# Full-array products in a two-block transformer kernel: score products with the queries' low parts on 128 rows, state products of the recurrence on 128 columns

## The chip, the cores and the metric

One core of a Trainium2 chip runs the whole program. The metric is the device time of one execution in microseconds. Three runs of the kernel before took 2723.95, 2730.51 and 2730.61 us; their median is 2730.51 us.

## The reference, cut to what matters

The network has a first block of two layers (mixers, convolutions and feed-forward nets over 512 tokens of width 1024) and a second block that mixes three things over the same 512 tokens: sparse attention with six heads in two groups (NSA), a recurrence with four heads (RWKV-7), and block attention with six heads (MoBA). All heads have 64 channels. The change touches only the second block's mixer. At 512 tokens every block is selected, so the attention parts are causal softmax attention, and NSA's window covers all tokens too.

```python
def _moba_mixer(p):
    q, k, v = [jnp.transpose(t.reshape(b, s, MOBA_HEADS, HEAD_DIM), (0, 2, 1, 3)) for t in _split_2(p, [D_MOBA] * 3)]
    ...
        s_o = jnp.einsum('bhqd,bhkd->bhqk', qc, ko)
        prob = _masked_softmax(jnp.concatenate([s_g, s_o], axis=-1) * scale, mask).astype(v.dtype)
        return jnp.einsum('bhqk,bhqkd->bhqd', prob[..., :n_g], vg) + jnp.einsum('bhqk,bhkd->bhqd', prob[..., n_g:], vo)
...
def _rwkv7_mixer(p, mu, w0, w2, a0, a2, g2, k_k, k_a, r_k, lnx_w, lnx_b):
    ...
    def step(state, inp):
        r_t, w_t, k_t, v_t, kk_t, a_t = inp
        sa = jnp.einsum('bhvk,bhk->bhv', state, -kk_t)
        state = state * w_t[:, :, None, :] + sa[..., None] * (kk_t * a_t)[:, :, None, :] + v_t[..., None] * k_t[:, :, None, :]
        return state, jnp.einsum('bhvk,bhk->bhv', state, r_t)
    ...
```

Everything is in float32. The kernel reaches that precision in the large products by splitting each operand into a high part (rounded to the format that TensorE takes in one pass) and a low part (the rest).

## The kernel before

`run` goes through the stages in order: first mixer, feed-forward net, conformer, second feed-forward net, then `mixer2` (the second block's mixer), then the last feed-forward net. The query tiles of `mixer2`'s attention are made from 1922.4 us on, and its score products run from 1951.8 to 2296.2 us. In `mixer2` three generators are interleaved: the attention (`attention`, with its projections `att_ft` and `att_tok`), the recurrence (`rwkv_blocks`) and the first half of the output projection (`wout_half`). Constants such as `RW_EVERY` and `WO_SHARE` say in which proportion they are interleaved. The building framework then sets the order of each engine's instructions by costs of its own; within an engine the order is fixed in the program.

**Score products.** For a block of 128 queries (`tb` from 0 to 3) and one head, the scores over the first `w = 128 (tb + 1)` keys are three products that accumulate in one bank of PSUM (lines 1967 to 1969, in `att_unit`). A key tile holds, for one head, the high parts of the 64 channels in one half of the 128 partitions and their low parts in the other half. A query tile `qp` (made by `att_q`, lines 1852 to 1862) has 128 columns for each of two heads with the high parts of the queries in both halves, so L1967 multiplies the high queries by high and low keys at once, on all 128 rows of TensorE's array. L1968 adds the low queries times the high keys, on the 64 rows of the half that has the high keys. L1969 adds the causal mask, on 128 rows. Each `qp` tile takes two ScalarE casts (L1859), two ScalarE copies to the other half (L1860) and two GpSimd subtractions that make the low parts (L1861). There are 24 such tiles, 12 for MoBA and 12 for NSA, and 72 score groups: 18 for each width of 128, 256, 384 and 512 keys.

**The recurrence.** A block of 128 tokens is worked in two halves of 64 (`c` in `rwkv_state`). In each half four products with the state `ST` (128 rows, two pairs of heads, two left sides) write `pu`; their left side is the 64 columns of the half's tokens, so they use 64 columns of the array and write 64 partitions (L1746). VectorE makes `U` from them (L1747), ScalarE copies the output part (L1748), and then products on 64 rows add to `pSr` (L1753, L1754), from which VectorE and GpSimd make the next state (L1757, L1759).

In the names of the profile, MATMUL and LDWEIGHTS carry the part of the array that they use: 64\*128 is 64 rows and 128 columns, 128\*64 is 128 rows and 64 columns. A float32 product that is not split has two records for each instruction.

Of the kernel before, what the change touches and what calls it, by code (L numbers as in the profile page):

```python
# [17 lines left out]
P = 128  # L18
# [294 lines left out]
class Kern:  # L313
# [1386 lines left out]
    def rwkv_state(self, pr, b):  # L1700

        nc, rp = self.nc, self.rwp
        mm = nc.tensor.matmul
        V = nc.vector
        hs = [slice(0, 64), slice(64, 128)]
        hd = [(p, h) for p in range(2) for h in range(2)]
        tk = lambda nm, p, b, h, tp=slice(0, P): pr[p][4][nm][tp, b, hs[h]]
        TT, MT, PT, QT = self.inv
        if b == 0:

            self.ST = [rp.tile([P, 2, P], F32, name=f"ST{j}") for j in range(2)]
            for j in range(2):
                nc.gpsimd.memset(self.ST[j], 0.0)
            self.oall = self.wp.tile([P, 2, T], F32, name="oall", tag="wh", bufs=3)
        o5 = self.oall.rearrange("p q (b h c) -> p q b h c", b=4, h=2)

        pair = lambda t, p: t.rearrange("p (q h) c -> p q (h c)", h=2)[:, p]
        own = lambda t, h: t.rearrange("p (q h) c -> p q h c", h=2)[:, :, h, 64 * h:64 * h + 64]
        pm = self.x("pmv", (P, 4, P))
        for i, (p, h) in enumerate(hd):  # L1720
            mm(pm[:, i], MT[:, i], pr[p][4]["v"][:, b], start=True, stop=True)
        mv = rp.tile([P, 4, 64], F32, name="mv", tag="mu", bufs=1)
        for h in range(2):
            nc.scalar.copy(mv.rearrange("p (q h) c -> p q h c", h=2)[:, :, h], own(pm, h))
        p1 = self.x("pt1", (P, 2, P))
        for i, (p, h) in enumerate(hd):
            mm(p1[hs[h], p], tk("al", p, b, h), TT[:, i], start=True, stop=True)
        t1 = rp.tile([P, 2, P], F32, name="t1")
        nc.scalar.copy(t1, p1)
        p2 = self.x("pt2", (P, 4, P))  # L1730
        for i, (p, h) in enumerate(hd):
            mm(p2[:, i], TT[:, i], pair(mv, p), start=True, stop=True)
        t2 = rp.tile([P, 2, P], F32, name="t2")
        for h in range(2):
            V.tensor_copy(t2[:, :, hs[h]], own(p2, h))
        yield
        U = rp.tile([P, 2, P], F32, name="U", tag="mu", bufs=1)
        for c in range(2):
            tp = hs[c]
            ts = slice(b * P + c * 64, b * P + c * 64 + 64)  # L1740
            ST, new = self.ST
            pu = self.x("pu", (P, 2, 2, P))
            for z in range(2):
                for p in range(2):
                    l = t1[:, p, c * 64:(c + 1) * 64] if z == 0 else pr[p][0][:, 1, ts]
                    mm(pu[tp, z, p], l, ST[:, p], start=True, stop=True)  # L1746
            V.scalar_tensor_tensor(U[tp], pu[tp, 0], -1.0, t2[tp], op0=OP.mult, op1=OP.add)  # L1747
            nc.scalar.copy(o5[tp, :, b].rearrange("p q h c -> p q (h c)"), pu[tp, 1])  # L1748
            if b < 3 or c < 1:
                pS = self.x("pSr", (P, 2, P))  # L1750
                for p in range(2):
                    tok = pr[p][4]
                    mm(pS[:, p], tok["kt"][tp, b], tok["v"][tp, b], start=p == 0, stop=False, skip_group_check=True)  # L1753
                    mm(pS[:, p], tok["b"][tp, b], U[tp, p], start=False, stop=p == 1, skip_group_check=True)  # L1754
                sw = rp.tile([P, 2, 64], F32, name="sw")
                for h in hs:
                    V.tensor_add(sw[h], ST[h, :, h], pS[h, :, h])  # L1757
                for h, e in zip(hs, (V, nc.gpsimd)):
                    e.tensor_mul(new[h, :, h], sw[h], self.wc[h, :, 2 * b + c:2 * b + c + 1].to_broadcast([64, 2, 64]))  # L1759
                self.ST = [new, ST]  # L1760
            yield
        po = self.x("po", (P, 4, P))
        for i, (p, h) in enumerate(hd):
            mm(po[:, i], QT[:, i], pr[p][4]["v"][:, b], start=True, stop=False)
            mm(po[:, i], PT[:, i], U[:, p], start=False, stop=True)
        for h in range(2):
            V.tensor_add(o5[:, :, b, h], o5[:, :, b, h], own(po, h))
        yield
# [83 lines left out]
    def att_q(self, q, tile):  # L1852

        nc = self.nc
        t = tile("qp", F32R)
        for j in range(2):
            a, b = slice(64 * j, 64 * j + 64), slice(64 - 64 * j, 128 - 64 * j)
            h = slice(j * P, j * P + P)
            nc.scalar.copy(t[a, h], q[a])  # L1859
            nc.scalar.copy(t[b, h], t[a, h])  # L1860
            nc.gpsimd.tensor_sub(t[a, 2 * P:3 * P], q[a], t[a, h])  # L1861
        return t

    def att_tok(self, part):
# [85 lines left out]
    def att_unit(self, tb, qk, one, v, gate, out, add=False):  # L1950
# [3 lines left out]
        nc, ap = self.nc, self.attp  # L1954
        w = (tb + 1) * P
# [6 lines left out]
        for j, (q, h, k) in enumerate(qk):  # L1962
            if j == 0 or not pair:
                pt = self.acc()
            p = pt[:, j * pair * w:j * pair * w + w]
            a = slice(64 * h, 64 * h + 64)
            nc.tensor.matmul(p, q[:, h * P:h * P + P], k[:, :w], start=True, stop=False, skip_group_check=True)  # L1967
            nc.tensor.matmul(p, q[a, 2 * P:3 * P], k[a, :w], start=False, stop=False, skip_group_check=True)  # L1968
            nc.tensor.matmul(p[:, tb * P:], self.identr, self.mneg, start=False, stop=True, skip_group_check=True)  # L1969
            ps.append(p)  # L1970
            if not pair:
                nc.vector.reduce_max(mx[:, j:j + 1], p, axis=AX.X)
            elif j:
                nc.vector.reduce_max(mx, pt[:, :2 * w].rearrange("p (j w) -> p j w", j=2), axis=AX.X)
            yield 0.2 * (tb + 1)
# [14 lines left out]
        for j0 in range(0, 2, m):  # L1990
            p = self.acc()
# [5 lines left out]
            t = self.t("peT")  # L1997
# [5 lines left out]
        p = self.acc()  # L2003
        for i, (t, s) in enumerate(tt):
            j, b = divmod(i, tb + 1)
            nc.tensor.matmul(p[:, P * j:P * j + P], t[:, s], v(j, b)[0], start=i == 0, stop=i == 2 * tb + 1,  # L2006
                             skip_group_check=True)
        for j in range(2):
            o = out if one else out[:, 64 * j:64 * j + 64]
            c = P * j + v(j, 0)[1]  # L2010
            a = p[:, c:c + 64]
# [428 lines left out]
```

## Time and profile before

| what | value |
|---|---|
| median of three runs | 2730.51 us |
| profiled execution | 2720.59 us, of which the span of instructions is 2718.9 us |
| TensorE (PE) busy | 2608.4 us, 96% of the span |
| VectorE (DVE) busy | 1832.1 us, 67% |
| ScalarE (ACT) busy | 1150.7 us, 42% |
| GpSimd (POOL) busy | 784.5 us, 29% |
| mean granted TensorE clock | 0.984 |

The profile names instructions by engine, source line and tiles. PEld is the queue of TensorE's weight loads, which can run beside the products. The start of a record is when the engine took it up; the time from one start to the next is what a product costs in a stream, and it is shorter than the record's own duration, since products are pipelined.

### The profile page before, as it was taken

The numbers are of one execution on the slowest core, as the hardware profiler recorded it, in microseconds if no ns is written. First come the engines' busy times: TensorE is split into PE (matmuls) and PEld (weight loads), VectorE is DVE, ScalarE is ACT, GpSimd is POOL, SyncE is SP. The second block draws the span as 40 slices with busy tenths as digits, with TensorE's granted clock in tenths as the row PEclk, the third lists the DMA queues.
The fourth block names the chain that finished last, engine by engine and source line by source line (L and its number), as shares of the span: only waits on it lengthen the run. The fifth ranks groups of instructions, "written<-read, shape, count | busy, mean of one in ns | idle before, by whom it ended". The sixth has DMA issues, their size and how long they took to land.

```text
span 2718.9 us, 37608 instructions
## 1 busy us (share of the span) xinstructions
PE 2608.4 (96%) x14088; PEld 2178.6 (80%) x14088; DVE 1832.1 (67%) x3234; ACT 1150.7 (42%) x2072; POOL 784.5 (29%) x767
## 2 busy tenths in 40 slices
PE   7999999999999999998789999999999999999998
PEld 3877778889778888787678888888787878988887
DVE  4686775775778888768998888657534666644422
ACT  3365543333424333228656433326535334533322
POOL 2132321222343111335754311342222002322231
PEclk8999999999999999999899999999999999999999
DMA  6112115341353333841012333333223001433332
GB/s 241 49 40 70 39 55 171 124 135 45 118 177 109 98 97 105 265 142 63 31 47 63 97 98 96 91 95 104 70 73 92 17 9 55 125 93 101 91 98 75
DMA packets 89367, 255.84 MB, mean 94 GB/s; under 512 B 10336, under 2 KB 14752, under 8 KB 89184
## 3 DMA queue, kind: packets, MB, share of 16 engines
q1 hardware_dynamic: 82320, 240.51, 28.3%
q0 software_dynamic: 2112, 6.29, 0.7%
q10 hardware_dynamic: 4752, 6.63, 0.7%
q8 instruction: 111, 1.82, 0.3%
q14 instruction: 72, 0.59, 0.1%
HBM read 245.00 MB, written 7.34 MB: 93 GB/s over the span
## 4 chain that ended last, share of the span: by engine, by line
PE 79%; DVE 12%; ACT 4%; issue 3%; DMA 2%; POOL 1%; DVEq 0%; POOLq 0%; SPq 0%; ACTq 0%
PE acc L402 19%; PE acc L404 19%; PE acc L403 19%; DVE cv L1470 2%; PE pa L1152 2%; PE acc L2006 1%; DVE e L972 1%; DVE wl L393 1%; DMA adaraw<-in_ada 1%; PE acc L1881 1%; PE acc L1968 1%; PE pr L618 1%; PE acc L1995 1%; PE ptm L1695 1%; PE acc L1969 1%
## 5 line engine op out<-in xcount | busy, mean ns | idle before, releaser
L402 PE MATMUL acc<-xh,wl 128*128 128x512 f32 (+2 forms) x2056 | 778.5, 380 | 16.2 <-DVE wl L393 7.4
L404 PE MATMUL acc<-xl,wh 128*128 128x512 f32 (+2 forms) x2056 | 765.0, 375 | 3.0 <-DVE xl L724 1.3
L403 PE MATMUL acc<-xh,wh 128*128 128x512 f32 (+2 forms) x2056 | 766.3, 374 | 0.0
L394 POOL TENSOR_TENSOR wl<-wraw,wh 128x256 fp32r<-128x256 f32 (+3 forms) x330 | 355.1, 1077 | 1181.7 <-ACT wh L391 1044.0
L391 ACT CAST wh<-wraw 128x1024 fp32r<-128x1024 f32 (+3 forms) x330 | 338.7, 1028 | 552.4 <-PE acc L404 320.2
L393 DVE TENSOR_TENSOR wl<-wraw,wh 128x768 fp32r<-128x768 f32 (+3 forms) x330 | 364.3, 1105 | 178.3 <-ACT wh L391 146.5
L402 PEld LDWEIGHTS acc<-xh,wl 128*128 128x128 f32 (+1 forms) x2056 | 391.7, 191 | 81.8 <-DVE wl L393 8.9
L404 PEld LDWEIGHTS acc<-xl,wh 128*128 128x128 f32 (+1 forms) x2056 | 389.2, 191 | 74.7 <-issue 1.9
L403 PEld LDWEIGHTS acc<-xh,wh 128*128 128x128 f32 (+1 forms) x2056 | 391.9, 191 | 56.9 <-issue 1.4
L2358 DVE SCALAR_TENSOR_TENSOR cacc<-acc,pk,cacc 128x441 f32<-128x441 f32 (+2 forms) x352 | 243.6, 692 | 28.0 <-ACT cacc L2349 18.6
L402 PE MATMUL acc<-gh,wl 128*128 128x512 f32 (+1 forms) x594 | 220.2, 371 | 0.0
L404 PE MATMUL acc<-gl,wh 128*128 128x512 f32 (+1 forms) x594 | 219.2, 369 | 0.0
L403 PE MATMUL acc<-gh,wh 128*128 128x512 f32 (+1 forms) x594 | 219.1, 369 | 0.0
L655 DVE SCALAR_TENSOR_TENSOR adaacc<-adaraw,sv,adaacc 128x512 f32<-128x512 f32 x140 | 116.7, 837 | 32.0 <-DMA adaraw<-in_ada 30.0
L404 PEld LDWEIGHTS acc<-gl,wh 128*128 128x128 f32 x594 | 111.4, 188 | 21.2
L403 PEld LDWEIGHTS acc<-gh,wh 128*128 128x128 f32 x594 | 111.4, 188 | 21.0
L402 PEld LDWEIGHTS acc<-gh,wl 128*128 128x128 f32 x594 | 111.4, 188 | 21.1
L1470 DVE SCALAR_TENSOR_TENSOR cv<-up,pk,cv 128x512 f32<-128x512 f32 x104 | 121.4, 1181 | 3.7 <-ACT cv L1444 1.5
L2302 DVE SCALAR_TENSOR_TENSOR cacc<-acc,pk,cacc 128x511 f32<-128x511 f32 (+1 forms) x44 | 32.9, 749 | 70.0 <-ACT cacc L2300 69.2
L1142 ACT COPY kcur<-kk 128x512 f32<-128x512 f32 x56 | 37.3, 665 | 94.5 <-DVE kk L1166 94.4
L1152 PE MATMUL pa<-qq,kcur 128*128 128x128 f32 x448 | 64.7, 288 | 5.8 <-DVE qq L1164 5.4
L2360 ACT ACTIVATE cacc<-cacc 128x512 f32<-128x512 f32 x44 | 27.8, 632 | 95.4 <-DVE cacc L2358 95.4
(671 smaller groups left out, 4679.3 us busy)
## 6 DMA issues: line engine op xcount, KB each, us to landing
wraw<-in_wup SPq DMA_DIRECT2D x132, 512.0 KB, 3.6
adaraw<-in_ada SPq DMA_DIRECT2D x160, 256.0 KB, 3.5
wraw<-in_wdn SPq DMA_DIRECT2D x48, 512.0 KB, 3.6
wraw<-in_wc SPq DMA_DIRECT2D x24, 512.0 KB, 3.7
wraw<-in_wdn SPq DMA_DIRECT2D x24, 384.0 KB, 3.1
wraw<-in_ada SPq DMA_DIRECT2D x16, 512.0 KB, 5.4
wraw<-in_wf SPq DMA_DIRECT2D x16, 512.0 KB, 3.7
wraw<-in_wo SPq DMA_DIRECT2D x16, 512.0 KB, 3.7
```

The lines of the kernel that those rows point to most:

```text
L391: nc.scalar.copy(wh[:, :n], raw[:, :n])
L393: nc.vector.tensor_sub(wl[:, :c], raw[:, :c], wh[:, :c])
L394: nc.gpsimd.tensor_sub(wl[:, c:n], raw[:, c:n], wh[:, c:n])
L402: mm(acc, wl, xh, start=first, stop=False)
L403: mm(acc, wh, xh, start=False, stop=False)
L404: mm(acc, wh, xl, start=False, stop=last)
L655: nc.vector.scalar_tensor_tensor(a, r, self.sv[:, k, 0:1], a, op0=OP.mult, op1=OP.add)
L1142: nc.scalar.copy(t.rearrange("p (a b c) -> p a b c", b=2, c=m), self.alt(kk, 0)(m))
L1152: mm(pa[:, s], kcur[:, s], self.alt(qq, 1)(m, c * P, P), start=True, stop=True)
L1470: nc.vector.scalar_tensor_tensor(acc, up[:, j:j + T], w(j), acc, op0=OP.mult, op1=OP.add)
L2302: nc.vector.scalar_tensor_tensor(a[:, d:], pg[:, :T - d], self.col("gcw", (2 - d) * KF + j), a[:, d:], op0=OP.mult, op1=OP.add)
L2358: nc.vector.scalar_tensor_tensor(o, g3[:, r0 + dy:r1 + dy, c0 + dx:c1 + dx], w, o, op0=OP.mult, op1=OP.add)
```

## The change

In `att_q` a second subtraction for each head writes the low parts of the queries into the other half of the partitions as well, and the low parts of the two heads now have 128 columns each (columns 256 to 512 of the tile) instead of sharing 128. L1968 then uses all 128 rows: it adds low queries times high keys, and also low queries times low keys. In `rwkv_state` the four products with the state take the full 128 tokens of the block as left side and write all 128 partitions of `pu`; what reads `pu` is unchanged and takes the same 64 partitions as before.

```diff
@@ rwkv_state
             tp = hs[c]
-            ts = slice(b * P + c * 64, b * P + c * 64 + 64)
             ST, new = self.ST
             pu = self.x("pu", (P, 2, 2, P))
             for z in range(2):
                 for p in range(2):
-                    l = t1[:, p, c * 64:(c + 1) * 64] if z == 0 else pr[p][0][:, 1, ts]
-                    mm(pu[tp, z, p], l, ST[:, p], start=True, stop=True)
+
+                    l = t1[:, p] if z == 0 else pr[p][0][:, 1, b * P:(b + 1) * P]
+                    mm(pu[:, z, p], l, ST[:, p], start=True, stop=True)
@@ att_q
-            h = slice(j * P, j * P + P)
+            h, l = slice(j * P, j * P + P), slice((2 + j) * P, (3 + j) * P)
             nc.scalar.copy(t[a, h], q[a])
             nc.scalar.copy(t[b, h], t[a, h])
-            nc.gpsimd.tensor_sub(t[a, 2 * P:3 * P], q[a], t[a, h])
+            nc.gpsimd.tensor_sub(t[a, l], q[a], t[a, h])
+            nc.gpsimd.tensor_sub(t[b, l], q[a], t[a, h])
@@ att_unit
-            a = slice(64 * h, 64 * h + 64)
             nc.tensor.matmul(p, q[:, h * P:h * P + P], k[:, :w], start=True, stop=False, skip_group_check=True)
-            nc.tensor.matmul(p, q[a, 2 * P:3 * P], k[a, :w], start=False, stop=False, skip_group_check=True)
+            nc.tensor.matmul(p, q[:, (2 + h) * P:(3 + h) * P], k[:, :w], start=False, stop=False, skip_group_check=True)
             nc.tensor.matmul(p[:, tb * P:], self.identr, self.mneg, start=False, stop=True, skip_group_check=True)
```

The number of TensorE instructions stays the same; GpSimd gets 48 subtractions more. The new subtraction is line 1862 of the changed kernel. The framework's order changes at a few places. On GpSimd's queue the subtractions double where they stand. The rows before, at the place where query tiles of NSA (`ftq`) and of MoBA (`mq`) are made close together, with the shapes of the output behind the names:

```order
L1861 TENSOR_TENSOR qp<-ftq_17365,qp 64x128 x2
L1861 TENSOR_TENSOR qp<-mq,qp 64x128 x4
L1861 TENSOR_TENSOR qp<-ftq_17244,qp 64x128 x2
L1861 TENSOR_TENSOR qp<-mq,qp 64x128 x4
L1861 TENSOR_TENSOR qp<-ftq_17297,qp 64x128 x2
```

In the changed kernel the third row above and the first half of the fourth have become these (ftq_17254 is the same tile as ftq_17244 before):

```order
L1861 TENSOR_TENSOR qp<-ftq_17254,qp 64x128
L1862 TENSOR_TENSOR qp<-ftq_17254,qp 64x128
L1861 TENSOR_TENSOR qp<-ftq_17254,qp 64x128
L1862 TENSOR_TENSOR qp<-ftq_17254,qp 64x128
L1861 TENSOR_TENSOR qp<-mq,qp 64x128
L1862 TENSOR_TENSOR qp<-mq,qp 64x128
L1861 TENSOR_TENSOR qp<-mq,qp 64x128
L1862 TENSOR_TENSOR qp<-mq,qp 64x128
```

Each tile's low parts are made head by head, so the second head's are complete only at the fourth subtraction, and a MoBA tile stands behind four subtractions of an NSA tile instead of two.

On TensorE's queue the second state product of the first block (`b` 0, `c` 1) was one group before:

```order
L1695 MATMUL ptm<-rwny,TT 128x128 x4
L1746 MATMUL pu<-ST_17920,t_17937 64x128 x2
L1746 MATMUL pu<-ST_17920,ar_16138 64x128
L1746 MATMUL pu<-ST_17920,ar_16245 64x128
L1753 MATMUL pSr<-tokv_16221,tokkt_16242 128x128
L2086 MATMUL acc<-ident,ya 128x128 x3
```

In the changed kernel its fourth product stands further back, with the update of the state behind it:

```order
L1695 MATMUL ptm<-rwny,TT 128x128 x4
L1746 MATMUL pu<-ST_17946,t_17963 128x128 x2
L1746 MATMUL pu<-ST_17946,ar_16138 128x128
L2086 MATMUL acc<-ident,ya 128x128 x3
L1967 MATMUL acc<-k,qp 128x128
...
L1995 MATMUL acc<-ident,pe 128x128 x2
L2086 MATMUL acc<-ident,ya 128x128 x3
L1746 MATMUL pu<-ST_17946,ar_16245 128x128
L1753 MATMUL pSr<-tokv_16221,tokkt_16242 128x128
```

So the fourth product moves behind two score groups and their neighbours. The other seven groups of state products stay whole and stay between the same neighbours, but for the sixth, which now has one product of L2006 instead of four between it and `pSr`.

## Rows read from the trace of the kernel before

**Rows 1.** The page's first part: busy time, share of the span, instructions of each engine

```profile
PE 2608.4 (96%) x14088; PEld 2178.6 (80%) x14088; DVE 1832.1 (67%) x3234; ACT 1150.7 (42%) x2072; POOL 784.5 (29%) x767
```

**Rows 2.** Windows: us, busy PE, PEld, DVE, ACT, POOL (records), clock, DMA share, GB/s

```profile
1950.00:2300.00 350.00, 341.18 (x2187) 280.30 (x2186) 197.76 (x636) 152.35 (x418) 64.55 (x98) 0.99 0.17 52
2150.00:2200.00 50.00, 49.05 (x321) 40.90 (x320) 33.55 (x123) 16.71 (x48) 2.01 (x4) 0.93 0.02 6
```

**Rows 3.** TensorE's waits from 1945 to 2300: total us, times, longest

```profile
PE pto L1816 <- DVE oall L1808: 2.0, 1, 2.0
PE acc L1967 <- ACT qp L1860: 1.2, 2, 0.6
...
PE pp L1668 <- DVE QT L1671: 0.4, 2, 0.2
```

**Rows 4.** Line 1968: duration ns min/median/max, first and last start, forms

```profile
L1968 PE MATMUL acc<-k,qp x72: 322/410/686, 1951.8 to 2296.2; 64*128 64x128 f32 x18, 64*128 64x256 f32 x18, 64*128 64x384 f32 x18, 64*128 64x512 f32 x18
```

**Rows 5.** Timeline of PE, a score group of 512 keys: start us, duration us, instructions

```profile
2278.82 0.39 PE L1967 MATMUL acc<-k,qp 128*128 128x512 f32 x1
2279.14 0.49 PE L1968 MATMUL acc<-k,qp 64*128 64x512 f32 x1
2279.56 0.33 PE L1969 MATMUL acc<-mneg,identr 128*128 128x128 f32 x1
2279.72 2.00 PE L2006 MATMUL acc<-vt,peT 128*128 128x128 f32 x16
```

**Rows 6.** Timeline of PEld, the same place; idle time before, in brackets

```profile
2279.14 0.18 PEld L1968 LDWEIGHTS acc<-k,qp 64*128 64x128 f32 x1 [0.25 <-issue]
2279.56 0.19 PEld L1969 LDWEIGHTS acc<-mneg,identr 128*128 128x128 f32 x1 [0.24 <-issue]
2279.66 1.87 PEld L2006 LDWEIGHTS acc<-vt,peT 128*128 128x128 f32 x16
```

**Rows 7.** Timeline of PE, a stream of full-array products of 512 columns

```profile
1954.09 0.40 PE L404 MATMUL acc<-xl,wh 128*128 128x512 f32 x1
1954.32 0.39 PE L402 MATMUL acc<-xh,wl 128*128 128x512 f32 x1
```

**Rows 8.** Timeline of PE, score groups of 384, 256 and 128 keys, and what follows

```profile
2089.15 0.39 PE L1967 MATMUL acc<-k,qp 128*128 128x384 f32 x1
...
2090.00 0.66 PE L2006 MATMUL acc<-vm,peT 128*128 128x128 f32 x4
...
2152.96 0.33 PE L1967 MATMUL acc<-k,qp 128*128 128x256 f32 x1
...
2153.70 1.11 PE L2006 MATMUL acc<-vt,peT 128*128 128x128 f32 x8
...
2078.54 0.28 PE L1967 MATMUL acc<-k,qp 128*128 128x128 f32 x1
...
2079.16 1.55 PE L2006 MATMUL acc<-vm,peT 128*128 128x128 f32 x12
```

**Rows 9.** Timeline of PE, state products of the last half block, and what follows

```profile
2281.65 0.65 PE L1746 MATMUL pu<-ST,t 128*64 128x128 f32 x4
...
2282.67 0.39 PE L402 MATMUL acc<-xh,wl 128*128 128x256 f32 x1
2282.89 0.28 PE L403 MATMUL acc<-xh,wh 128*128 128x256 f32 x1
2283.01 0.27 PE L404 MATMUL acc<-xl,wh 128*128 128x256 f32 x1
```

**Rows 10.** Line 1861: duration ns min/median/max, first and last start, form

```profile
L1861 POOL TENSOR_TENSOR qp<-mq,qp x24: 447/456/972, 1922.4 to 2091.6; 64x128 fp32r<-64x128 f32 x24
```

**Rows 11.** Timeline of POOL, two neighbouring query tiles

```profile
2086.61 0.98 POOL L1861 TENSOR_TENSOR qp<-ftq,qp 64x128 fp32r<-64x128 f32 x2 [3.58 <-ACT qp L1859]
2087.66 0.98 POOL L1861 TENSOR_TENSOR qp<-mq,qp 64x128 fp32r<-64x128 f32 x2
```

**Rows 12.** Timeline of PE, the score products that use the second of these tiles

```profile
2088.24 0.44 PE L1967 MATMUL acc<-k,qp 128*128 128x384 f32 x1 [0.61 <-ACT qp L1860]
2088.62 0.44 PE L1968 MATMUL acc<-k,qp 64*128 64x384 f32 x1
```

## The prediction, as put on record before the run

> **What bounds the kernel now.** I read the page's busy times first: TensorE is busy in 96% of the span [rows 1], so time is found in its queue or nowhere. The stretch that the change touches comes next, by the table of windows: from 1950 to 2300 us, where all 72 low score products and all state products lie, TensorE is busy for 341.2 of 350 us, VectorE for 197.8, ScalarE for 152.4 and GpSimd for 64.6 [rows 2]. The list of TensorE's waits in that stretch confirms it: nine entries, the longest 2.0 us, the last 0.4 us, none of them on GpSimd [rows 3]. So here the time is the sum of TensorE's steps, a step being the time from one product's start to the next one's.
>
> The timeline then shows what steps cost. In a stream of full-array products of 512 columns a step is 1954.32 - 1954.09 = 0.23 us [rows 7]; of 256 columns 2283.01 - 2282.89 = 0.12 us [rows 9]; of 128 columns 0.11 us, since 16 weight loads of 0.19 us span 1.87 us, or 1.68 us for 15 steps [rows 6]. A score group does not keep to this. At 512 keys L1967 takes a step of 0.32 us, L1968 0.42 and L1969 0.16 [rows 5]. The queue of weight loads tells why: the load of L1968 starts only at 2279.14, together with its product, after 0.25 us in which the queue waited for nothing that the profile shows, and the same happens at L1969 [rows 6]. In the full-array stream loads run ahead beside the product before. So a change of the array's shape, 128\*128 to 64\*128 and back, makes the engine finish the product (about 0.09 us on top of 0.23) and then exposes the next load (another 0.10 us at L1968). That is two changes in each score group.
>
> **The change part by part.** Profiled times go with their own execution, 2720.6 us; the median of the runs, 2730.5, is 9.9 us above it, and I apply the difference to the median.
>
> Low score products: after the change all three products of a group have the same shape, so I cost them at stream steps. There are 18 groups of each width [rows 4].
> - 512 keys: 2279.72 - 2278.82 = 0.90 us now [rows 5], 0.23 + 0.23 + 0.11 = 0.57 then, 0.33 saved.
> - 384 keys: 2090.00 - 2089.15 = 0.85 us now [rows 8]; a step of 384 columns lies between 0.12 and 0.23, I take 0.17, so 0.45 then, 0.40 saved.
> - 256 keys: 0.74 us now [rows 8], 0.12 + 0.12 + 0.11 = 0.35 then, 0.39 saved.
> - 128 keys: 0.62 us now [rows 8], 0.33 then, 0.29 saved.
>
> The sum is 18 x 1.41 = 25.4 us. Bounds: 72 times the smallest, 20.9, and 72 times the largest, 28.8.
>
> State products: eight groups of eight records. In the one shown they take 2282.67 - 2281.65 = 1.02 us where eight steps of 0.11 are 0.88, so 0.14 too much; the L402 behind it takes 0.22 instead of 0.12, 0.10 too much [rows 9]; and the 16 products of L2006 ahead of it take 2281.65 - 2279.72 = 1.93 us [rows 5, 9], 0.17 more than 16 x 0.11, of which I count 0.10 for the change of shape. A group with full-array neighbours on both sides gives back 0.34. Five of the eight are followed by L1753 on 64 rows, where a change of shape stays; they give 0.10 ahead and 0.04 of the 0.14, the exposed first load. That is 3 x 0.34 + 5 x 0.14 = 1.7 us. The wider weights cost nothing that I can see: 64-column records average 1.02/8 = 0.13 us with their switches and 128-column ones 0.11. The move of one state product behind two score groups delays a state that is next used only when the following block begins; I cost it at nothing, with at most the 2.0 us of the longest wait now if that cover failed.
>
> GpSimd: 48 subtractions of 0.45 us [rows 10] are 22 us more on an engine that is idle for 285 us of the stretch, so by busy time they are free. By latency they are not everywhere. At 2087.66 a MoBA tile's subtractions start and its product L1968 begins at 2088.62 [rows 11, 12], 0.96 us later. With subtractions every 0.52 us (two take 0.98), the NSA tile ahead occupies GpSimd until 2088.7, and the MoBA tile's two heads are complete at 2089.7 and 2090.8. Behind the waiting product stand the mask, the second head's group and the L2006 that starts at 2090.00 now [rows 8]; that start would come near 2091.1 instead of the 2089.2 that two groups of 0.45 us behind 2088.24 would give. So this place costs 1.9 us. I take 3 us for all places of this kind: most tiles are made several us before their use (NSA's far more), and only MoBA's late tiles are made so close. Bounds: 1.9 us, and 12 MoBA tiles at 0.7 us, 8.4.
>
> New waits: TensorE idles for 350 - 341.2 = 8.8 us here now, and its work shrinks by 27 us while the chains through VectorE and ScalarE keep their lengths. L1967 already waits twice for the ScalarE copies, 0.6 us each [rows 3, 12]. I take 2 us more; bounds 0 and 8.8, twice the idle time of now.
>
> The clock: from 2150 to 2200 it was granted at 0.93 on average [rows 2], so about 7 us at 1.2 GHz instead of 2.4. What it follows from I cannot read here. If this stretch vanishes, up to 3.5 us come back; I count nothing.
>
> Sum: 25.4 + 1.7 - 3 - 2 = 22.1 us. 2720.6 - 22.1 = 2698.5 for an execution like the profiled one, and 2730.5 - 22.1 = 2708.4 us by the median.
>
> **A rule that speaks against it.** The trace shows loads of full-array products starting while the full-array product before still runs: in the stream of 16, loads of 0.19 us start every 0.11 us [rows 6]. The Trainium skill (TensorE: Matmul & The Clock Gate, Part 3, The mechanism) says that a weight load overlaps running products only where its row group differs. By that rule the loads of the changed L1968 would stay exposed; the trace of before does not agree, though no run here has yet shown two score products in this shape. The time that it would give is the third rival.
>
> **The rivals.**
> - The feeders take over. The queries' casts, GpSimd's subtractions and the softmax chain come just in time more often, and TensorE waits for what it has gained: 27.1 - 8.8 - 8.4 = 9.9 us are left, 2720.6. For it: the waits of L1967 on ScalarE. Against: GpSimd and ScalarE idle for more than half of the stretch.
> - The other side: GpSimd becomes the bound. Where VectorE works beside it a subtraction took 0.97 instead of 0.45 us [rows 10]. If all did, a tile would be complete 2 x 0.97 = 1.9 us later; if TensorE waited for this at all 24 tiles, 46.6 us would be lost against 27.1 gained, 2750.0. The change is slower by more than 0.3% from (27.1 + 8.2)/24 = 1.5 us of waiting for each tile on. Against: TensorE waited for GpSimd nowhere [rows 3].
> - Loads do not overlap on the same rows. Then 0.10 us at each L1968 (0.42 against 0.32) and 0.05 at each L1969 (0.16 against 0.11) stay [rows 5], 10.8 us in all: 27.1 - 10.8 - 5 = 11.3, 2719.2 us.
> - The change does not do what it says: L1968 is slow for another cause than its shape, for instance as a product whose weights GpSimd wrote. Then only the 5 us of new waits are left, 2735.5, no change that can be told. Against: L402 behind the state products shows the same 0.10 us and has nothing of GpSimd's in it [rows 9].
>
> **How the numbers follow.** The forecast has 0.76, the first rival 0.13, the second 0.03, the third 0.04, the fourth 0.04. A difference under 0.3%, 8.2 us, cannot be told from no change here: faster means below 2722.3. Most of the forecast and nearly all of rivals one and three lie there, 0.88; no change 0.09 (rival four and the weak ends of one and three), slower 0.03. The range: the largest gain is 28.8 + 1.7 + 3.5 - 1.9 = 32.1, 2698.4; at the other end the smallest, 20.9 + 1.7 - 8.4 - 5 = 9.2, gives 2721.3.
>
> **What would show it.** L1968 has the form 128\*128, and its step is 0.23 us at 512 keys and 0.12 at 256; L1967's at 512 keys falls from 0.32 to 0.23; the idle time of the load queue before L1968 and L1969 is gone. The stretch from the first score group to the last shrinks by about 22 us and the stages before and after keep their lengths. TensorE's waits list GpSimd for the first time, for some 3 us near the MoBA tiles of the last head pair. The prediction is wrong if L1968 keeps a step of 0.42 us at 512 keys, or if TensorE's waits in the stretch grow by more than 10 us.

## The result, and the profile after

The changed kernel takes 2700.96 us (median of four runs, 2698.73 to 2704.91); the kernel before, run four times beside it, takes 2729.68 us (2723.95 to 2730.61). The ratio is 0.9898, with a 95% interval of 0.9881 to 0.9915: faster. The forecast was 2708.4 us and its range, as worked out there, 2698.4 to 2721.3, so the time lies inside. In two later sessions the changed kernel ran again, with ratios of 0.991 (0.989 to 0.993) and 0.9898 (0.988 to 0.9917). The profiled execution took 2700.14 us, 20.5 less than the profiled one of before.

The first part of the page answers to [rows 1]:

```profile
PE 2588.3 (96%) x14088; PEld 2183.7 (81%) x14088; DVE 1832.5 (68%) x3234; ACT 1150.0 (43%) x2072; POOL 808.1 (30%) x815
```

TensorE's busy time fell by 20.1 us with the same number of instructions, and GpSimd's rose by 23.6 with 48 more. The span fell by 20.5, so nearly everything that TensorE gained went through to the end.

Line 1968 of the changed kernel, in the form of [rows 4] (duration ns, first and last start us, forms; then who released the engine after idle time):

```profile
L1968 PE MATMUL acc<-k,qp x72: 272/335/687, 1954.4 to 2277.5; 128*128 128x128 f32 x18, 128*128 128x256 f32 x18, 128*128 128x384 f32 x18, 128*128 128x512 f32 x18
its engine sat idle before it (us, times) until:
  POOL qp L1862: 3.9, 6
```

All 72 low products now have the form 128\*128. From the first to the last of them it is 323.1 us, where it was 344.4 [rows 4]: 21.3 us less. The stages ahead of it and behind it keep their length, 2374.5 us before and 2375.3 after. The last line is new: it adds up four loads (2.5 us) and two products (1.4 us) that stood idle until a GpSimd subtraction was done. The two products wait at the same moments as two of the loads (2080.57 and 2086.30 us), so the 3.9 us count these twice; the four places come to 2.5 us.

Score groups of 512 keys, TensorE's products and then its weight loads (start us, duration us); the places answer to [rows 5] and [rows 6]:

```profile
2262.10 0.40 PE L1967 MATMUL acc<-k,qp 128*128 128x512 f32 x1
2262.34 0.39 PE L1968 MATMUL acc<-k,qp 128*128 128x512 f32 x1
2262.57 0.22 PE L1969 MATMUL acc<-mneg,identr 128*128 128x128 f32 x1
2262.63 2.00 PE L2006 MATMUL acc<-vt,peT 128*128 128x128 f32 x16
2264.46 0.61 PE L1746 MATMUL pu<-ST,t 128*128 128x128 f32 x4
...
2265.28 0.36 PE L402 MATMUL acc<-xh,wl 128*128 128x256 f32 x1
2265.48 0.28 PE L403 MATMUL acc<-xh,wh 128*128 128x256 f32 x1
```

```profile
2262.11 0.19 PEld L1968 LDWEIGHTS acc<-k,qp 128*128 128x128 f32 x1
2262.34 0.19 PEld L1969 LDWEIGHTS acc<-mneg,identr 128*128 128x128 f32 x1
```

Read the starts downwards. L1967 takes a step of 0.24 us (0.32 before), L1968 0.23 (0.42), L1969 0.06 (0.16): 0.53 us for the group instead of 0.90. Both groups are among the fastest of their width; the medians, further down, are 0.60 and 1.00. The load of L1968 starts 0.23 us ahead of its product, beside L1967, where it used to start together with it. The brackets of [rows 6], 0.25 and 0.24 us of "issue", are gone.

The same over the whole stretch is seen in the list of the load queue's waits, from 1945 to 2300 us (total us, times, longest). Before:

```profile
PEld acc L1968 <- issue: 10.2, 44, 0.4
PEld acc L1969 <- issue: 7.7, 35, 0.3
```

After, neither of the two rows exists; the largest entry is another one:

```profile
PEld acc L1968 <- POOL qp L1862: 2.5, 4, 1.2
```

So 17.9 us in which the load queue stood still "for nothing" vanished, and 2.5 us of waiting for GpSimd came in.

Some of TensorE's own waits after, in the window of [rows 3] (total us, times, longest):

```profile
PE acc L2006 <- ACT peT L1999: 1.8, 2, 1.4
...
PE acc L1968 <- POOL qp L1862: 1.4, 2, 1.0
```

The sum over the stretch without its ends (columns as in [rows 2]):

```profile
1955.00:2275.00 320.00, 307.61 (x2125) 269.12 (x2124) 188.67 (x611) 146.50 (x403) 79.70 (x136) 0.99 0.17 51
```

TensorE is idle for 320 - 307.6 = 12.4 us, where it was idle for 8.8 of 350 [rows 2]; before, from 1955 to 2295 us, it is 8.8 as well.

And the place at which the prediction put the new wait, first TensorE, then GpSimd (the bracket is the idle time before and what ended it); it answers to [rows 11] and [rows 12]:

```profile
2084.90 0.45 PE L1967 MATMUL acc<-k,qp 128*128 128x384 f32 x1 [0.61 <-ACT qp L1860]
2086.30 0.48 PE L1968 MATMUL acc<-k,qp 128*128 128x384 f32 x1 [0.96 <-POOL qp L1862]
...
2087.35 0.69 PE L1968 MATMUL acc<-k,qp 128*128 128x384 f32 x1
...
2087.94 1.16 PE L2006 MATMUL acc<-vm,peT 128*128 128x128 f32 x4
```

```profile
2083.26 0.45 POOL L1861 TENSOR_TENSOR qp<-ftq,qp 64x128 fp32r<-64x128 f32 x1 [2.75 <-ACT qp L1859]
...
2085.30 0.45 POOL L1861 TENSOR_TENSOR qp<-mq,qp 64x128 fp32r<-64x128 f32 x1
2085.80 0.45 POOL L1862 TENSOR_TENSOR qp<-mq,qp 64x128 fp32r<-64x128 f32 x1
...
2086.84 0.45 POOL L1862 TENSOR_TENSOR qp<-mq,qp 64x128 fp32r<-64x128 f32 x1
```

Four subtractions of the NSA tile stand ahead of the MoBA tile's. The first head's low part is complete at 2086.25 and its product starts at 2086.30; the second head's at 2087.29, its product at 2087.35. From L1967 to L2006 it is 3.04 us; the prediction's figures were 2091.1 - 2088.24 = 2.9.

### The profile page after: what moved, and what is told of

It is laid out like the page before. It is cut to its first block, busy times and chain, and to the rows that moved or that the text cites. A ratio compares the mean times of both kernels' runs of the same rounds, so it can differ in the third digit from the quotient of the medians.

```text
span 2698.4 us, 37649 instructions
## 1 busy us (share of the span) xinstructions
PE 2588.3 (96%) x14088; PEld 2183.7 (81%) x14088; DVE 1832.5 (68%) x3234; ACT 1150.0 (43%) x2072; POOL 808.1 (30%) x815
## 3 DMA queue, kind: packets, MB, share of 16 engines
q1 hardware_dynamic: 82320, 240.51, 28.7%
## 5 line engine op out<-in xcount | busy, mean ns | idle before, releaser
L402 PE MATMUL acc<-xh,wl 128*128 128x512 f32 (+2 forms) x2056 | 779.8, 380 | 17.2 <-DVE wl L393 7.2
L404 PE MATMUL acc<-xl,wh 128*128 128x512 f32 (+2 forms) x2056 | 765.0, 375 | 1.7 <-POOL xl L376 0.8
L402 PEld LDWEIGHTS acc<-xh,wl 128*128 128x128 f32 (+1 forms) x2056 | 392.5, 191 | 82.0 <-DVE wl L393 8.4
L404 PEld LDWEIGHTS acc<-xl,wh 128*128 128x128 f32 (+1 forms) x2056 | 389.4, 191 | 72.6 <-issue 1.7
L402 PE MATMUL acc<-gh,wl 128*128 128x512 f32 (+1 forms) x594 | 221.3, 372 | 0.0
L404 PE MATMUL acc<-gl,wh 128*128 128x512 f32 (+1 forms) x594 | 220.4, 371 | 0.0
L404 PEld LDWEIGHTS acc<-gl,wh 128*128 128x128 f32 x594 | 112.6, 189 | 21.3
L402 PEld LDWEIGHTS acc<-gh,wl 128*128 128x128 f32 x594 | 112.5, 189 | 21.0
L1168 POOL TENSOR_TENSOR tot<-tot 128x256 f32<-128x256 f32 (+5 forms) x48 | 26.0, 541 | 147.5 <-DVE qq L1164 136.4
```

The source lines that it names most:

```text
L402: mm(acc, wl, xh, start=first, stop=False)
L404: mm(acc, wh, xl, start=False, stop=last)
```

## The experiments

Every run below is timed in rounds beside the kernel before on the same chip; ratios are to that kernel, with 95% intervals. "Stage" is the time from the first to the last start of the score groups' first product in the run's profile: 344.3 us before, 323.0 after. Where an expectation names 323.5 or 323.6, it counts to the last mask; where one names 3.9 us of waits on GpSimd, two places are in it twice.

**The changed kernel again.** No edit.

> The changed kernel once more, timed in five rounds beside the kernel before, to settle the size: its medians differ by 28.7 us, its two profiled executions by 20.5 us. Theory (shape changes alone, as priced from steps): the stage from the first score group to the last shrinks by about 21.6 us as in the first profile, and the two kernels differ by 20 to 24 us. Rival (something outside the stage, such as the stretches at 1.2 GHz, gives the rest): they differ by 27 us or more again, and the stage shrinks by no more than 22 us.

2700.92 us against 2725.62 (17 runs, 2715.03 to 2732.82): 0.991 (0.989 to 0.993). Stage 323.2. The 24.7 us lie between the theory's 20 to 24 and the rival's 27. This is the yardstick of the next three.

**Only the score products.** `att_q` and L1968 as in the changed kernel, state products as before.

```diff
-            nc.gpsimd.tensor_sub(t[a, 2 * P:3 * P], q[a], t[a, h])
+            nc.gpsimd.tensor_sub(t[a, l], q[a], t[a, h])
+            nc.gpsimd.tensor_sub(t[b, l], q[a], t[a, h])
-            nc.tensor.matmul(p, q[a, 2 * P:3 * P], k[a, :w], ...)
+            nc.tensor.matmul(p, q[:, (2 + h) * P:(3 + h) * P], k[:, :w], ...)
```

> Only the low score products on 128 rows, with their second subtraction on GpSimd; the state products as before. Theory: 72 groups give back 0.33 to 0.40 us each, less the waits on GpSimd, so L1968 has a step of about 0.23 us at 512 keys, and the kernel is 19 to 25 us faster than before, over nine tenths of the whole change. Rival (the state products carry much of it): under 15 us.

2702.57 us, ratio 0.9917 (0.9896 to 0.9937), stage 323.8. Within the noise the score products do all of it.

**Only the state products.**

```diff
-                    l = t1[:, p, c * 64:(c + 1) * 64] if z == 0 else pr[p][0][:, 1, ts]
-                    mm(pu[tp, z, p], l, ST[:, p], start=True, stop=True)
+                    l = t1[:, p] if z == 0 else pr[p][0][:, 1, b * P:(b + 1) * P]
+                    mm(pu[:, z, p], l, ST[:, p], start=True, stop=True)
```

> Only the state products on 128 columns; query tiles and score products as before. Theory: 1.7 us by steps, up to 3 with the products just ahead, so no difference that five rounds can tell (within 0.2%). Rival (waits behind the state products are shortened, since U comes earlier): 5 us or more faster.

2723.59 us, ratio 0.9991 (0.9975 to 1.0006), stage 343.8. The predicted 1.7 us is below what the runs can tell. The profile shows both parts where they were expected: in the changed kernel eight state products take 2265.28 - 2264.46 = 0.82 us (1.02 before [rows 9]), L402 behind them 0.20 (0.22) and the 16 products ahead 1.83 (1.93).

**The shape without the subtractions.** The kernel before, where L1968 uses all 128 rows but takes the high parts of the queries again; the low parts are left out of the sum, and GpSimd makes no more of them than before.

```diff
-            nc.tensor.matmul(p, q[a, 2 * P:3 * P], k[a, :w], ...)
+            nc.tensor.matmul(p, q[:, h * P:h * P + P], k[:, :w], ...)
```

> L1968 on 128 rows, but with the high parts of the queries once more as weights, so the low parts are left out of the scores; GpSimd has only its 48 old subtractions and nothing waits for them. The state products are as before. Theory: the shape alone gives 25 us (72 groups at 0.33 to 0.40), and the difference to the kernel with the new subtractions is what TensorE waited for GpSimd, 2 to 5 us, so 23 to 28 us faster than before. Rival (L1968 was slow because GpSimd wrote its weights): its step stays at 0.42 us at 512 keys only where the low parts are its weights, so this one gains as well, but then the changed kernel could not have a step of 0.23; rival (full-array loads do not overlap): about 14 us.

2699.53 us, ratio 0.9897 (0.9875 to 0.9919), stage 323.1. The shape alone gives the whole gain: not the other contents, nor the other columns of the tile. Taking GpSimd's waits away brings little more: the stage is 0.7 us shorter than that of the score products alone (323.8), and TensorE's idle time from 1955 to 2275 us 1.4 us (12.3 against 13.7). The longest of TensorE's waits for ScalarE in this run, from 1945 to 2300 us:

```profile
PE acc L2006 <- ACT peT L1999: 2.2, 2, 1.5
PE acc L1995 <- ACT pe L1983: 1.6, 2, 0.9
```

GpSimd is gone from the list, and the same head pair shows where much of the time stays (timeline of TensorE):

```profile
2081.77 0.44 PE L1967 MATMUL acc<-k,qp 128*128 128x384 f32 x1 [0.61 <-ACT qp L1860]
2082.05 0.34 PE L1968 MATMUL acc<-k,qp 128*128 128x384 f32 x1
...
2089.70 0.49 PE L2006 MATMUL acc<-vm,peT 128*128 128x128 f32 x2 [0.68 <-ACT peT L1999]
```

The two groups run without the 0.96 us of waiting for GpSimd, TensorE comes sooner to what ScalarE makes, and waits there.

**Half the changes of shape.** The kernel before, with the products of the two groups of a unit in another order: high, mask, high, mask, low, low. The low products stay on 64 rows. Where the two groups share a bank (NSA, 128 and 256 keys), the second group's first product now opens the bank ahead of the first group's low product, which changes the sum there; all products are issued.

```diff
-            nc.tensor.matmul(p, q[a, 2 * P:3 * P], k[a, :w], start=False, stop=False, ...)
-            nc.tensor.matmul(p[:, tb * P:], self.identr, self.mneg, start=False, stop=True, ...)
+            nc.tensor.matmul(p[:, tb * P:], self.identr, self.mneg, start=False, stop=False, ...)
...
+        for j, (q, h, k) in enumerate(qk):
+            a = slice(64 * h, 64 * h + 64)
+            p = ps[j]
+            nc.tensor.matmul(p, q[a, 2 * P:3 * P], k[a, :w], start=False, stop=True, ...)
```

> The kernel before, but the order inside a unit of two score groups is high, mask, high, mask, low, low, with the low products still on 64 rows: two changes of shape in each unit instead of four, nothing more on GpSimd, state products as before. Theory (each change of shape costs, not the 64 rows): NSA's units, whose two low products use the same half, give back half of 2 x 0.36 us, and the second of two low products has its load run ahead; MoBA's, on different halves, the same or more if the two overlap (then their steps of 0.42 us at 512 keys fall to near zero for one of them). 36 units at 0.36 us or more: 12 to 18 us faster than before. Rival (the 64-row shape itself is slow): less than 5 us, with a step of 0.42 us at 512 keys for both low products.

2711.63 us against 2726.49 (23 runs), ratio 0.9943 (0.9921 to 0.9964), stage 330.3: 14.9 us of gain, rather more than half of the changed kernel's (24.7 to 28.7). Two units of 512 keys (the low products are L1975 here), first of NSA, whose two products use the same 64 rows, then of MoBA, where they use different halves:

```profile
2257.93 0.73 PE L1975 MATMUL acc<-k,qp 64*128 64x512 f32 x2
2258.59 2.05 PE L2011 MATMUL acc<-vt,peT 128*128 128x128 f32 x16
...
2060.16 0.49 PE L1975 MATMUL acc<-k,qp 64*128 64x512 f32 x2
2060.58 0.64 PE L1919 MATMUL acc<-cw,zp 128*62 128x256 f32 x2
```

NSA's two low products take 2258.59 - 2257.93 = 0.66 us, MoBA's two 2060.58 - 2060.16 = 0.42, as much as one alone did before [rows 5]. By the records MoBA's start 3 to 4 ns apart: they run side by side, so at MoBA's 12 of the 36 units more than a change of shape is saved.

**Both products on 64 rows.** The kernel before with L1967 on the same half as L1968; high queries times low keys are left out.

```diff
-            nc.tensor.matmul(p, q[:, h * P:h * P + P], k[:, :w], start=True, ...)
+            nc.tensor.matmul(p, q[a, h * P:h * P + P], k[a, :w], start=True, ...)
```

> The kernel before with L1967 on 64 rows as well (the same half as L1968), which leaves the products of high queries and low keys out of the scores. The number of changes of shape stays two for each group, now ahead of L1967 and behind L1968. Theory: L1967 to L1968 has no change, so L1967 loses its finishing time but its own load is exposed; the low product's step falls from 0.42 to about 0.32 us at 512 keys (finishing alone), the time from a group's start to its end and the kernel's time stay the same within 4 us. Rival (64 rows are slow in themselves): L1967 takes 0.42 us too, and the kernel is 5 to 8 us slower.

2726.62 us, ratio 1.0002 (0.9986 to 1.0017), stage 353.7. The timeline of a group of 512 keys with the product ahead of it, then the weight loads:

```profile
2292.06 0.28 PE L404 MATMUL wo<-xl,wh 128*128 128x256 f32 x1
2292.27 0.49 PE L1967 MATMUL acc<-k,qp 64*128 64x512 f32 x1
2292.60 0.39 PE L1968 MATMUL acc<-k,qp 64*128 64x512 f32 x1
2292.93 0.33 PE L1969 MATMUL acc<-mneg,identr 128*128 128x128 f32 x1
2293.09 2.00 PE L2006 MATMUL acc<-vt,peT 128*128 128x128 f32 x16
```

```profile
2292.27 0.18 PEld L1967 LDWEIGHTS acc<-k,qp 64*128 64x128 f32 x1
2292.38 0.19 PEld L1968 LDWEIGHTS acc<-k,qp 64*128 64x128 f32 x1
```

Each of the two products on the same 64 rows has a step of 0.33 us, but the load of L1968 starts 0.22 us ahead of its product, beside L1967: loads do overlap on the same 64 rows. Both steps are the stream's 0.23 us and the cost of one change: L1967's load is exposed behind the change ahead of it, and L1968 is finished ahead of the change behind it, as the theory had it. The group is shorter than before (2293.09 - 2292.27 = 0.82 us against 0.90), yet the time is not, since now the product ahead of the group has to finish too: L404 has a step of 2292.27 - 2292.06 = 0.21 us, where its stream has 0.12 [rows 9]. Equal neighbours on one side only move the two changes; what counts here is how many there are. The long stage of this profile, the slowest of the kernel's ten runs, goes with the clock: from 1955 to 2295 us 0.95 of full was granted on average, against 0.99 before.

**Only the subtractions.** The kernel before, with a second subtraction whose result nothing reads.

```diff
+            nc.gpsimd.tensor_sub(t[b, 3 * P:4 * P], q[a], t[a, h])
```

> The kernel before with the 48 new subtractions on GpSimd, into columns that nothing reads; the products as before. Theory: they are hidden but for a few places where L1968 needs a tile just behind them, so 0 to 4 us slower, not to be told from no change. Rival (GpSimd becomes the bound or slows VectorE): 8 us slower or more.

2729.04 us, ratio 1.001 (0.9991 to 1.0028), stage 348.5. So 48 subtractions more cost GpSimd 22 us and the program nothing that the times can tell. From 1955 to 2295 us GpSimd is busy for 77.69 us, and TensorE waits for it once, for 0.5 us. The stage is 4.2 us longer than before; most of that goes with the clock, which was granted at 0.98 in that stretch against 0.99 (see the table behind the last experiment).

**The new subtraction on VectorE.** The changed kernel, with one word different, run in two sessions.

```diff
-            nc.gpsimd.tensor_sub(t[b, l], q[a], t[a, h])
+            nc.vector.tensor_sub(t[b, l], q[a], t[a, h])
```

> The changed kernel with the second subtraction of each head on VectorE instead of GpSimd. Theory from the second set of runs: the waits of L1968 on GpSimd (3.9 us) go, but the kernel with high parts again had none of them and its stage was as long as the changed kernel's, 323.6 us, since TensorE waits a little later instead; so it stays within 3 us of the changed kernel. Rival (waits on GpSimd count in full): 4 us faster than the changed kernel, with VectorE's 48 x 0.2 us hidden.

2696.43 us, ratio 0.9898 (0.9878 to 0.9918), stage 322.6.

> The changed kernel again, beside the three versions below on the same chip, as their base: 22 to 29 us faster than the kernel before, as in its first two timings, with a stage of 323.5 us.

> The second subtraction on VectorE, once more: its median was 4.5 us below that of the changed kernel, timed on another occasion, while its profiled stage was only 0.5 us shorter (323.05 against 323.5). Theory: within 2 us of the changed kernel. Rival (the waits on GpSimd count): 3 to 5 us faster again.

Side by side on one chip, the changed kernel took 2697.16 us (0.9898, 0.988 to 0.9917) and this one 2696.98 (0.9893, 0.9874 to 0.9912), against 2725.16 for the kernel before; they can't be told apart. (Both stages are 322.1 us.) TensorE's waits for GpSimd are gone from the second one's list, and its waits for ScalarE's `pe` have grown from 1.0 to 2.1 us; its idle time from 1955 to 2275 us is 11.1 us against 13.1.

**The same cure at another place.** NSA's products with the compressed keys (L2034) also use 64 rows, six behind each mask. On top of the VectorE version the compressed keys get a zero half, so that they use 128 rows.

```diff
-        self.kcmp = ap.tile([P, 32], F32, name="kcmp")
+        self.kcmp = ap.tile([P, 2, 32], F32, name="kcmp")
...
-                nc.tensor.matmul(s3[:, r], self.ft[f"q{r}"][gs, ts], self.kcmp[gs], ...)
+                nc.tensor.matmul(s3[:, r], self.ft[f"q{r}"][:, ts], self.kcmp[:, g], ...)
```

> The same, and the products of queries with compressed keys (L2034, 48 of 32 columns) on 128 rows as well, with a key tile for each head whose other half is zero. Theory (changes of shape cost, wherever they stand): 16 changes fewer, at about 0.1 us for the finishing and up to 0.1 for the exposed load, 1.6 to 3 us less in the stage than with the subtraction on VectorE alone, which a median can hardly tell. Rival (only the score groups gain): the stage stays at 323 us.

2695.36 us, ratio 0.9895 (0.9878 to 0.9912), stage 320.6: 1.5 us less than the VectorE version's 322.1, and not to be told in the times. The stage settles nothing either, since the VectorE version's had 10.2 us at the lower clock and this one 3.4 (table below). The timeline of one mask with its six records, in the changed kernel and in this one:

```profile
2121.71 0.29 PE L2031 MATMUL acc<-mcmp,identr 128*128 128x96 f32 x1
2121.93 0.85 PE L2034 MATMUL acc<-kcmp,ftq 64*128 64x32 f32 x6
2122.72 0.31 PE L2031 MATMUL acc<-mcmp,identr 128*128 128x96 f32 x1
```

```profile
2120.73 0.29 PE L2032 MATMUL acc<-mcmp,identr 128*128 128x96 f32 x1
2120.86 0.82 PE L2035 MATMUL acc<-kcmp,ftq 128*128 128x32 f32 x6
2121.51 1.14 PE L1683 MATMUL pyy<-Tm,NT 128*128 128x128 f32 x8
```

1.01 us became 0.78 at this place. With 8 such places an estimated 8 x 0.23 = 1.8 us would be gained; neither the times nor the stages show it.

**One transpose for three.** On top of that, the three transposes of 32 columns become one of 96, with three small copies behind it in place of one.

```diff
-            for r in range(3):
-                nc.tensor.transpose(p[:32, r * P:(r + 1) * P], e3[:, r], self.ident)
+            nc.tensor.transpose(p[:96, :P], e[:, :96], self.ident)
-            nc.scalar.copy(t[:32, :384], p[:32, :384])
+            for r, copy in enumerate((nc.scalar.copy, nc.vector.tensor_copy, nc.scalar.copy)):
+                copy(t[:32, r * P:(r + 1) * P], p[32 * r:32 * r + 32, :P])
```

> The same, and one transpose of 96 columns (a full array) instead of three of 32 for the compressed scores, with three small copies behind it instead of one. Theory: 13 changes of shape and 16 records of 0.11 us fewer, so 3 to 4.5 us less again in the stage, 5 to 7 us faster than the changed kernel in all, if the softmax chain of the compressed keys does not wait 0.5 us longer at each of eight copies. Rival (that chain ends late): no gain over the one before.

2701.39 us, ratio 0.9906 (0.9885 to 0.9926), stage 326.0: nothing gained, and not the 5 to 7 us that the theory had. It is the longest stage of the versions with full-array scores. Its profile has 2.5 us of waiting for ScalarE's `pe` (L1996), 0.6 in the version above, but also the lowest clock of these versions, and the clock is enough for the 5.4 us between the two, as follows.

**The clock in the stages.** The granted clock has two levels, 2.4 and 1.2 GHz, and how long a stage ran at the lower one differs from profile to profile. What that costs is seen in the run with both products on 64 rows, where a whole group of 512 keys ran at 1.2 GHz. From its start at 2252.12 to the next product's at 2253.54 us it took 1.42 us instead of 0.82, so an estimated 0.4 us are lost for each us at 1.2 GHz. With this the last column is an estimate of each stage at full clock:

| profile | stage, us | of it at 1.2 GHz | less 0.4 of that |
|---|---|---|---|
| kernel before | 344.3 | 6.8 | 341.6 |
| changed kernel | 323.0 | 6.8 | 320.3 |
| changed kernel again | 323.2 | 6.8 | 320.5 |
| changed kernel, third | 322.1 | 3.4 | 320.7 |
| only the score products | 323.8 | 3.4 | 322.4 |
| only the state products | 343.8 | 13.7 | 338.3 |
| shape without subtractions | 323.1 | 6.8 | 320.4 |
| half the changes of shape | 330.3 | 10.2 | 326.2 |
| both products on 64 rows | 353.7 | 34.1 | 340.1 |
| only the subtractions | 348.5 | 13.7 | 343.0 |
| subtraction on VectorE | 322.6 | 10.2 | 318.5 |
| the same again | 322.1 | 10.2 | 318.0 |
| compressed keys on 128 rows | 320.6 | 3.4 | 319.2 |
| one transpose for three | 326.0 | 17.1 | 319.2 |

The three profiles of the changed kernel come within 0.4 us of each other. The run with one transpose is as long as the one without, and the version with VectorE's subtraction is 2 to 3 us shorter than the changed kernel.

## Why the prediction was right

**What bounds it: right.** TensorE's steps were the time. Its busy time fell by 20.1 us and the span by 20.5.

**The low score products, 25.4 us: right in mechanism and in size.** The median time from L1967's start to the end of L1969's step, over the groups whose three records stand together in the trace (69 of 72 before, 67 after), fell from 0.65, 0.74, 0.86 and 1.00 us (128, 256, 384, 512 keys) to 0.37, 0.36, 0.50 and 0.60. That is 0.28, 0.38, 0.36 and 0.40 less: 18 x 1.42 = 25.6 us. The prediction's 512-key group was the fastest of its width. Its 0.33 for 512 keys was too low and its 0.40 for 384 too high; that these cancel is luck, but small. One step was mis-sized: L1969 behind 256 to 512 keys fell to 0.06 us and not to the 0.11 of a stream of 128-column products. L1967 at 512 keys fell from 0.32 to 0.23 only where its own load runs at least 0.11 us ahead (5 of 17 groups). It took 0.29 us with a lead of 0.06, 0.32 with 0.03 and 0.34 with none, and 0.09 more at each of these leads before; so the 0.09 us of finishing were given back at every lead, as counted.

The cause that was named, drained product and exposed load at a change of shape, is borne out from several sides: the queue's idle time before L1968 and L1969 (17.9 us) is gone; the full-array form with other contents gives the same time; half the changes of shape give rather more than half of the gain; as many changes at other places, with both products on 64 rows, give the same time as before. The Trainium skill (TensorEngine Tiling (Array Packing), Key Properties) says that a change of the tiling mode drains TensorE, though not what that costs; the trace agrees, and the cost here is what a group lost, 0.28 to 0.40 us for two changes around one product.

**Loads that do not overlap on the same rows: refuted**, for full-array products by the load of L1968 that starts 0.23 us ahead of its product while L1967 runs, and for products on the same 64 rows by the load that starts 0.22 us ahead. So the measurement decides against the rule that the prediction quoted from the Trainium skill (TensorE: Matmul & The Clock Gate, Part 3, The mechanism).

**GpSimd, -3 us: right in place, close in size.** The waits came at the MoBA tiles of the last head pair and sum to 2.5 us, the two that both the product and its load waited for counted once. Without them TensorE's idle time was 1.4 us shorter (high parts again, beside the score products alone) and 2.0 us shorter (VectorE's subtraction, beside the changed kernel), and by the table's estimate the stage was 2.0 and 2.7 us shorter. The times can't tell it (2696.98 against 2697.16 us side by side). Part of a removed wait comes back as a wait for ScalarE. GpSimd as the bound (2750.0 us) is refuted by the subtractions alone, which cost nothing that the times can tell.

**Change without effect, feeders that take over: refuted** by the result; of the latter a part is true, since TensorE's idle time in the stretch went from 8.8 to 12.4 us, 3.6 more where the sum had 5 for GpSimd and the other new waits.

**State products, 1.7 us:** seen in the profile's steps, not in the times (0.9991, 0.9975 to 1.0006). By the table's estimate the stage gained 3.3 us from them alone and 1.9 us on top of the score products.

**The size.** The sum of 22.1 us is what the profiles show: the stage fell by 21.3 us here, and by 21.1 and 22.2 in the two repeats. The forecast of 2708.4 is 7.4 us too high for another reason: it added to the profile's time the 9.9 us by which the kernel before's median lay above its profiled execution, as if that were a constant. The changed kernel's median lies 0.8 us above its own. The 9.9 us go with the clock: the profiled execution of before had a mean granted clock of 0.984, and of the kernel's 51 runs in the later sessions one had that, where the median was 0.979. Their times follow the clock, from 2735.2 us at 0.975 (median of two) to 2715.0 at 0.984 (one run).

By medians the gain was 28.7, 24.7 and 28.0 us, where the sum of 22.1 (a ratio of 0.9919) lies inside one of the three intervals and just above the other two. The 3 to 6 us more go with the clock too. The changed kernel's 11 runs in these sessions had a median of 0.981. At the same granted clock the two kernels differ by less:

| mean granted clock | kernel before: runs, median us | changed kernel: runs, median us | difference |
|---|---|---|---|
| 0.981 | 3, 2721.3 | 3, 2698.4 | 22.9 |
| 0.982 | 5, 2719.7 | 3, 2700.5 | 19.2 |

A straight line of time against clock through all 62 runs, with a step between the kernels, puts the step at 21.9 us (standard error 0.9), and the prediction's sum was 22.1. This is a fit and not an experiment: why the kernel before ran at a lower mean clock isn't shown. The prediction counted nothing for the clock, with up to 3.5 us in its range, and that is the term that was missing in its time.

## What to carry to other kernels

A lone product on half the rows between full-array products costs more than a full-array one: here 0.42 + 0.16 us instead of 0.23 + 0.06 with the mask behind it, since the queue of weight loads stops twice, and the product ahead of the change takes 0.09 us more. Look in the load queue's waits for idle time that nothing ended ("issue") ahead of a line whose shape differs from its neighbours'; zeros or useful extra rows that make the shapes equal remove it, and where that can't be done, put the odd shapes together, so that there are fewer changes. When a waiting engine's release is to be made faster, see first what it would wait for next: here part of the 2.5 us removed came back as waits for ScalarE, and the times can't tell the rest. And compare two profiled stages only with the time that each spent at the lower clock beside them: here that was 3.4 to 34.1 us and hid or feigned differences of several us.

## What was not expected of the hardware

- Two products on different halves of the rows, into different banks, started 3 to 4 ns apart and took 0.42 us together at 512 columns; two on the same half took 0.66.
- Loads overlap on the same 64 rows as they do in the full array: the second of two loads started 0.22 us ahead of its product. The steps of 0.33 us at 512 columns, where full-array products have 0.23, are the change ahead of the first and the change behind the second.
- A 128-column product behind one of 512 took a step of 0.06 us, less than the 0.11 of a stream of them. The product behind it takes more than in its stream: L402 behind a mask took 2276.35 - 2276.18 = 0.17 us in the changed kernel, where its stream has 0.12 (0.17 behind a mask in the kernel before, too).
- The spread of the kernel before over its runs, 2715 to 2737 us, was as wide as the gain, though the ratios came out to 0.2%. It follows the granted clock of each run, by 2.1 us for each 0.001.
